# Whole-head values' products of 512 columns, a gate turned by VectorE and probabilities scaled on ScalarE, in the attention stage of a fused diffusion block

## The chip, the cores and the metric

One core of one Trainium2 chip runs the whole block in one launch. The metric is the device time of an execution in microseconds; the kernel before has a median of 1329.95 us over three runs (1327.25 to 1331.77). TensorE multiplies, VectorE and ScalarE work on whole tiles, GpSimd (POOL) and SyncE (SP) issue DMAs, as ScalarE does too.

## The reference, cut to what matters

The input is 512 latent tokens and 256 context tokens, each of 2048 channels. All arithmetic is in float32. The part that the change touches:

```python
q = _rope(_rmsnorm(_heads(p, OFF_Q, N_Q_HEADS), q_norm_g[l]), cos, sin) * q_scale
k = _rope(_rmsnorm(_heads(p, OFF_K, N_KV_HEADS), k_norm_g[l]), cos, sin)
v = _heads(p, OFF_V, N_KV_HEADS)
attn = _attention(q, concatenate([k, kc]), concatenate([v, vc]))   # softmax(q k^T) v, 12 heads, 4 key heads
...
y_a = (attn * jax.nn.silu(z_a)) @ w_pa
y_b = (_fourier_mix(u_b) * jax.nn.silu(z_b)) @ w_pb
return (g_a * y_a + g_b * y_b) @ w_o
```

Ahead of this lies an adaptive normalisation and one input projection of 9216 columns, and behind it a gated residual and a final normalisation. There are 12 query heads of 128 channels, 4 key and value heads, 768 keys. `z_a` is the gate of the attention branch: 12 x 128 channels, one for each of the branch's.

## The kernel before, in words

Float32 precision is kept by splitting each operand into a high and a low part (`split_from`, L162: a copy on ScalarE gives the high part, a subtraction on VectorE the low one) and by three products for each pair (`mm3`, L303). `split_from` is thus one line for many tiles, L163 on ScalarE and L164 on VectorE.

The kernel runs in stages. First come the modulation and the Fourier branch. Then the input projection runs as eight column groups (`KINDS`, L58) by a scheme of seven products of half-size blocks (`Group`, L727). The first three groups each hold queries for four heads (`c` = 0 in `qz_done`, L887) and the gate for the same heads (`c` = 1). The queries are normalised and rotated, turned by VectorE in blocks of 32 x 32 (L872) and written to DRAM (`q_d`). The gate is put through `z * (tanh(z/2) + 1)`, which is twice its SiLU, and written to DRAM by head (`z_d`) with the tokens on the partitions.

The attention stage is a hand-written loop of 48 steps and 3 closing ones (L1220 to L1252). Step `i` works for query tile `t = i % 4` (128 tokens) of head `h = i // 4`:

- `load_head(h + 2)` (L1046) when `t` is 1: the gate by one POOL DMA (L1048), the queries by `load_turned` (L210), which is four SP DMAs whose pieces are 32 floats long (L215). It thereby finishes the transposition that VectorE began within 32 x 32 blocks.
- `scores(i)` (L1147): six products give 128 x 768 scores in PSUM (tag `x`, two buffers of two banks); VectorE takes the row maximum (L1157) and scales it (L1158); ScalarE takes the exponential into a tile `probs` and sums it (L1160).
- `fill(1)`: one unit (three products of 512 columns) of a filler, the Fourier branch's own projection, 64 units in all. A unit is handed out evenly: `want = 3 + 61 * (i + 1) // 48`. Every fourth unit ends with a ScalarE copy out of PSUM (L1134).
- `values` (L1183), in every second step from step 4: 18 products of 256 columns for two query tiles, two steps behind; the same PSUM bank takes two TensorE transposes of the gate (L1191), ScalarE copies those out (L1199) and VectorE multiplies (L1200). Behind the second half of a head the result is split into `S` (L1204), the left operand of the branch's projection.
- `turn(i - 1)` (L1172): six TensorE transposes of the probabilities into PSUM (`tp`, one buffer of two banks), then ScalarE and VectorE split them into `pth` and `ptl`. Two pairs of these buffers exist, each for 256 tokens.
- `divide(i - 1)` (L1164): VectorE takes the reciprocal of the row sum (L1169) and multiplies it into the gate's rows (L1170), not into the probabilities.
- `split_queries(h + 1)` when `t` is 1, and further units of the filler that are owed.

Which instruction stands where on an engine is decided by a scheduler at build time: each engine takes the earliest instruction of the program whose operands and buffers it reckons to be free. The trace shows such shifts: the products of step `i + 2`'s scores stand partly ahead of `turn(i)`. On the chip each engine runs its list in that order. A buffer with one copy makes its next writer wait for its last reader.

After the loop the branch's projection over all heads follows (`products`, L1207), of which six pieces already run in the last steps.

Of the kernel before, what the change touches and what calls it, by code (L numbers as in the profile page):

```python
# [10 lines left out]
F32 = mybir.dt.float32  # L11
F32R = mybir.dt.float32r
ACT = mybir.ActivationFunctionType
ALU = mybir.AluOpType
# [4 lines left out]
P = 128  # L19
D = 2048  # L20
T = 512
C = 256
KK = D // P
HD = 128
NH = 12
NKV = 4
GQ = NH // NKV
NKEY = T + C
KT = NKEY // P
# [29 lines left out]
NQZ, KV = 3, 5  # L59
# [48 lines left out]
def block_kernel(ctx, tc, xT, ctx_rows, ctx_toks, x, c_row, w_ss, w_gate, vecs, qkg, rope, dft_c, dft_s,  # L108
                 w_start, w_g, w_pab, w_o, final_g, out):
    nc = tc.nc  # L110
# [15 lines left out]
    dsc = ctx.enter_context(tc.tile_pool(name="dsc", bufs=1, space=DRAM))  # L126
# [2 lines left out]
    cf_d = dsc.tile([4, P, 7, 2, P], F32, name="cf_d")  # L129
    v_d = dsc.tile([NKV, P, KT, HD], F32, name="v_d")  # L130
    q_d = dsc.tile([NQZ, 4, P, 4 * P], F32, name="q_d")
    z_d = dsc.tile([NH, P, 4, HD], F32, name="z_d")
    b_d = dsc.tile([2, P, 2, T], F32, name="b_d")
    g_d = dsc.tile([2, 2, 4, P, 1024], F32, name="g_d")
    pss, ps = region("ps", None, space=PSUM)
# [3 lines left out]
    def uid(s):  # L139
        cnt[0] += 1  # L140
        return f"{s}{cnt[0]}"
# [20 lines left out]
    def split_from(src, hi, lo):  # L162
        nc.scalar.activation(hi, src, ACT.Copy)  # L163
        return nc.vector.tensor_tensor(lo, src, hi.bitcast(F32), op=ALU.subtract)  # L164
# [45 lines left out]
    def load_turned(dst, src, g):  # L210

        for c in range(4):
            n = P * g + 32 * c
            blocks = src[:, :, n : n + 32].rearrange("t (a i) j -> i (t a) j", a=4)
            nc.sync.dma_start(dst[32 * c : 32 * c + 32].rearrange("i (u j) -> i u j", j=32), blocks)  # L215
# [74 lines left out]
    def slot_tile(p, shape, dt):  # L290
        return p[0].tile([P] + list(shape), dt, tag=p[1], bufs=1, name=uid("s"))

    def take(shape, dt=F32, pool=None):
        p = next((p for p in free if p[0] is pool), free[0])
        free.remove(p)
        t = slot_tile(p, shape, dt)
        home[id(t)] = p, t
        return t

    def give(*ts):  # L300
        free.extend(home.pop(id(t))[0] for t in ts)

    def mm3(o, ah, al, bh, bl, start, stop, cont=False):  # L303

        nc.tensor.matmul(o, ah, bh, start=start, stop=False, skip_group_check=cont)  # L305
        nc.tensor.matmul(o, ah, bl, start=False, stop=False, skip_group_check=cont)  # L306
        nc.tensor.matmul(o, al, bh, start=False, stop=stop, skip_group_check=cont)  # L307


    ident = const.tile([P, P], F32, name="ident")  # L310
# [29 lines left out]
    kept = {}  # L340
# [21 lines left out]
    flat = lambda v: v.rearrange("p t c -> p (t c)")  # L362
# [14 lines left out]
    for g in range(LAST + 1):  # L377
        for name in ONE_GROUP:
# [6 lines left out]
            for pc in range(4):  # L385
                p = context_piece(g, name, pc)
# [12 lines left out]
    S = {}  # L399
# [3 lines left out]
    for name in OUT_GROUP:  # L403
        stream_product(name, 8, w_o[1], BY_DVE_OUT)
        if name in DONE:
            half, c = DONE[name]
# [480 lines left out]
    def qz_done(half, c, v, t):  # L887

        if c:
            e = pair("x" if half else "y")  # L890
            nc.scalar.activation(e, v, ACT.Tanh, scale=0.5)
            nc.vector.scalar_tensor_tensor(v, e, 1.0, v, op0=ALU.add, op1=ALU.mult)
            r = v.rearrange("p t (h d) -> p t h d", h=4)
            for b in range(2):
                nc.scalar.dma_start(z_d[4 * group.g : 4 * group.g + 4, :, 2 * half + b, :].rearrange("h p d -> p h d"), r[:, b])
        else:
            to = q_d[group.g]
            rotated(half, v, lambda: pair("y"), qss[group.g][:, 8 * half : 8 * half + 8], False,
                    lambda t, r: nc.scalar.dma_start(to[t].rearrange("p (h d) -> p h d", h=4), r))
# [14 lines left out]
    class Context:  # L914
# [43 lines left out]
        def values(self, b, v):  # L958
            nc.scalar.dma_start(by_group(v_d[:, :, 4 + b, :]), v.rearrange("p (g d) -> p g d", g=4))
# [84 lines left out]
    qz, qs, kv = {}, {}, {}  # L1044

    def load_head(h):  # L1046
        qz[h] = take((2, T))
        nc.gpsimd.dma_start(qz[h][:, 1, :], flat(z_d[h]))  # L1048
        load_turned(qz[h][:, 0, :], q_d[h // 4], h % 4)

    def get_keys(g):
        keys = get(("K", g))
        kv[g] = tuple(w[:, 0, :] for w in keys) + get(("V", g))
# [6 lines left out]
    for g, kind in enumerate(KINDS):  # L1060
# [8 lines left out]
        group = Group(g, forms, new_ev, {"qz": qz_done, "kv": kv_done, "gate": gate_done}[kind], {"a": "x", "b": "y", "c": "x"})  # L1069
# [36 lines left out]
    ats_, atp = region("atp", "right", reuse_waits="tile")  # L1106
# [5 lines left out]
    ybs, S = {}, {}  # L1112
# [31 lines left out]
    probs, pts, branch = {}, {}, {}  # L1144
    NSTEP = 4 * NH

    def scores(i):  # L1147
        h, t = divmod(i, 4)
        kh, kl = kv[h // GQ][:2]
        s = slice(t * P, (t + 1) * P)  # L1150
        qh, ql = qs[h][:, 0, s], qs[h][:, 1, s]
        sc = flat(pair("x"))
        for a, b in ((0, 512), (512, 768)):
            mm3(sc[:, a:b], qh, ql, kh[:, a:b], kl[:, a:b], True, True)
        mx = stats[:, 4 * (i % 4) : 4 * (i % 4) + 4]
        r = qss[h // 4][:, 4 * t + h % 4 : 4 * t + h % 4 + 1]
        nc.vector.tensor_reduce(mx[:, 0:1], sc[:, :NKEY], axis=AX.X, op=ALU.max, negate=True)  # L1157
        nc.vector.tensor_tensor(mx[:, 0:1], mx[:, 0:1], r, op=ALU.mult)  # L1158
        probs[i] = take((NKEY,))
        nc.scalar.activation(probs[i], sc[:, :NKEY], ACT.Exp, bias=mx[:, 0:1], scale=r, accum_out=mx[:, 1:2])  # L1160
        if t == 3:
            give(qs.pop(h))

    def divide(i):  # L1164

        h, t = divmod(i, 4)
        z = qz[h][:, 1, t * P : t * P + P]
        r = stats[:, 4 * (i % 4) + 2 : 4 * (i % 4) + 3]
        nc.vector.reciprocal(r, stats[:, 4 * (i % 4) + 1 : 4 * (i % 4) + 2])  # L1169
        nc.vector.tensor_scalar(z, z, r, None, op0=ALU.mult)  # L1170

    def turn(i):  # L1172
        p = probs.pop(i)
        tp = flat(psp.tile([P, 2, 512], F32, tag=f"y{turned_y}", bufs=1, name=uid("tp")))
        for k in range(KT):
            nc.tensor.transpose(tp[:, k * P : (k + 1) * P], p[:, k * P : (k + 1) * P], ident)
        if i % 2 == 0:
            pts[i // 2] = [atp.tile([P, KT, 256], F32R, tag=n, bufs=2, name=uid(n)) for n in ("pth", "ptl")]
        c = slice((i % 2) * P, (i % 2) * P + P)
        split_from(tp[:, :NKEY].rearrange("p (k q) -> p k q", k=KT), *(w[:, :, c] for w in pts[i // 2]))  # L1180
        give(p)

    def values(half):  # L1183
        h, second = divmod(half, 2)
        vh, vl = kv[h // GQ][2:]
        pth, ptl = pts.pop(half)
        av = b1()
        for k in range(KT):
            mm3(av[:, :256], vh[:, k, :], vl[:, k, :], pth[:, k, :], ptl[:, k, :], k == 0, k == KT - 1)
        for t in range(2):  # L1190
            nc.tensor.transpose(av[:, 256 + t * P : 256 + (t + 1) * P], qz[h][:, 1, (2 * second + t) * P : (2 * second + t + 1) * P], ident)  # L1191
        if second:
            give(qz.pop(h))
            if h % GQ == GQ - 1:
                give(*kept.pop(h // GQ))
        else:
            branch[h] = take((2, T))
        at, zt = (branch[h][:, i, 256 * second : 256 * second + 256] for i in range(2))
        nc.scalar.copy(zt, av[:, 256:])  # L1199
        nc.vector.scalar_tensor_tensor(at, av[:, :256], 0.5, zt, op0=ALU.mult, op1=ALU.mult)  # L1200
        if second:
            if h % 2 == 0:
                S[h // 2] = [take((2, T), F32R) for _ in range(2)]
            split_from(branch[h][:, 0, :], *(w[:, h % 2, :] for w in S[h // 2]))  # L1204
            give(branch.pop(h))

    def products(j, accs):  # L1207

# [7 lines left out]
                        pc == 0 and k == 0, pc == BRANCH_A[-1] and k == 1)  # L1216
                yield pc, t

    filled = 0
    for i in range(NSTEP + 3):  # L1220
        h, t = divmod(i, 4)
        if i < NSTEP:
            if t == 1 and h + 2 < NH:
                load_head(h + 2)
            if i == 24:
                load_row(0)
            elif i == 28:
                silu_of_row(0)
            if i % 12 == 10 and i // 12 + 1 < NKV:
                get_keys(i // 12 + 1)  # L1230
            scores(i)
        want = min(3 + 61 * (i + 1) // NSTEP, 64)
        if want > filled:
            fill(1)
            filled += 1
        if i % 2 == 0 and i >= 4:
            values((i - 4) // 2)
        if 1 <= i <= NSTEP:
            turn(i - 1)
            divide(i - 1)  # L1240
        if t == 1 and h + 1 < NH:
            split_queries(h + 1)
        if want > filled:
            fill(want - filled)
            filled = want
        if i == NSTEP - 1:
            fill(1)
            first_sums = [pair("x") for _ in range(2)]
            first = products(CHUNKS[0], first_sums)
        if NSTEP > i - 2 >= NSTEP - 3:  # L1250
            next(first)
            next(first)  # L1252
# [353 lines left out]
```

## Time and profile before

| | |
|---|---|
| median of three runs | 1329.95 us |
| profiled execution | 1326.24 us, its span 1324.5 us |
| granted TensorE clock | 0.997 |
| TensorE busy | 1291.6 us, 98% |
| VectorE busy | 983.3 us, 74% |
| ScalarE busy | 657.0 us, 50% |
| attention stage | 828 to 1027 us |

A row of the groups names line, engine, operation, output and inputs by their names in the program, shapes, count, then the busy time in us, the mean of one in ns, and the engine's idle time before them with what ended it. A row of the timeline starts with the start and the length in us, then engine, line, operation and count; a bracket gives the idle time ahead of it. Matmuls are pipelined, so the length of one (0.28 us for 256 columns) is more than the distance to the next one's start. `SPq` and `POOLq` are the queues that issue DMAs. `y<-pth,s` are the values' products, `y<-whi,s` the filler's, `x<-s,s` the scores'. A row of the windows gives the busy time of each engine in a stretch, its count of instructions in brackets, then clock, DMA share and GB/s.

### The profile page before, as it was taken

How to read it: one execution, taken by the hardware profiler on the slowest of the kernel's cores; microseconds unless marked ns; L12 is line 12 of the kernel's file. 1: busy time of each engine (PE TensorE's matmuls, PEld its weight loads, DVE VectorE, ACT ScalarE, POOL GpSimd, SP SyncE). 2: the span in 40 equal slices, each digit the busy share in tenths (PEclk: the TensorE clock that was granted, in tenths of full speed). 3: DMA queues.
4: the chain of work that ended last, by engine and by line, in shares of the span. 5: the costliest groups of instructions: out<-in, count | busy, mean ns of one | idle time of the engine just before them, and what ended most of it. 6: DMA issues, size and time to landing. Idle time of an engine off the chain costs nothing. (4 is left out here: it accounts for less than half of the span.)

```text
span 1324.5 us, 17511 instructions
## 1 busy us (share of the span) xinstructions
PE 1291.6 (98%) x6522; PEld 1053.6 (80%) x6522; DVE 983.3 (74%) x1341; ACT 657.0 (50%) x1018; POOL 136.4 (10%) x186
## 2 busy tenths in 40 slices
PE   7999999999999999999999999999999999999995
PEld 3566888888888887888888888888888888878884
DVE  4655889878777875748487667778776889687677
ACT  5322655555555553544354545767665133364534
POOL 1110011110201111011021010000000100110210
PEclk9999999999999999999999999999999999999999
DMA  9996677887898987977659798432113988778973
GB/s 382 404 383 250 222 194 204 217 231 214 198 306 214 280 275 199 306 180 171 203 153 329 226 220 211 100 90 80 33 49 128 350 346 301 185 155 252 225 204 127
DMA packets 125718, 291.28 MB, mean 220 GB/s; under 512 B 46784, under 2 KB 60608, under 8 KB 121280
## 3 DMA queue, kind: packets, MB, share of 16 engines
q1 hardware_dynamic: 88912, 176.10, 39.7%
q0 software_dynamic: 21168, 91.24, 28.6%
q10 hardware_dynamic: 15552, 22.81, 4.9%
q8 instruction: 51, 0.84, 0.3%
q14 instruction: 35, 0.29, 0.1%
HBM read 263.37 MB, written 26.75 MB: 219 GB/s over the span
## 5 line engine op out<-in xcount | busy, mean ns | idle before, releaser
L163 ACT ACTIVATE whi<-wr 128x1024 fp32r<-128x1024 f32 (+1 forms) x129 | 135.1, 1052 | 180.2 <-PE y L307 77.3
L306 PE MATMUL x<-wlo,s 128*128 128x512 f32 x548 | 214.4, 391 | 4.0 <-DVE wlo L164 4.0
L305 PE MATMUL y<-whi,s 128*128 128x512 f32 x544 | 214.3, 394 | 1.8 <-ACT s L774 1.1
L305 PE MATMUL x<-whi,s 128*128 128x512 f32 x548 | 214.6, 392 | 0.2 <-ACT s L771 0.2
L307 PE MATMUL x<-whi,s 128*128 128x512 f32 x548 | 214.0, 391 | 0.0
L306 PE MATMUL y<-wlo,s 128*128 128x512 f32 x544 | 212.3, 390 | 1.3 <-DVE wlo L164 1.3
L307 PE MATMUL y<-whi,s 128*128 128x512 f32 x544 | 212.3, 390 | 0.0
L164 DVE TENSOR_TENSOR wlo<-wr,whi 128x1024 fp32r<-128x1024 f32 (+1 forms) x129 | 155.6, 1212 | 63.4 <-ACT whi L163 63.0
L163 ACT ACTIVATE whi<-R 128x1024 fp32r<-128x1024 f32 x115 | 121.2, 1059 | 129.5 <-PE x L307 58.5
L164 DVE TENSOR_TENSOR wlo<-R,whi 128x1024 fp32r<-128x1024 f32 x115 | 140.0, 1221 | 48.7 <-ACT whi L163 48.5
L306 PEld LDWEIGHTS x<-wlo,s 128*128 128x128 f32 x548 | 103.2, 188 | 26.3 <-DVE wlo L164 5.1
L305 PEld LDWEIGHTS y<-whi,s 128*128 128x128 f32 x544 | 102.2, 188 | 24.4 <-DVE s L1200 2.8
L305 PEld LDWEIGHTS x<-whi,s 128*128 128x128 f32 x548 | 103.3, 189 | 22.1 <-ACT s L771 0.5
L307 PEld LDWEIGHTS x<-whi,s 128*128 128x128 f32 x548 | 103.2, 188 | 21.5
L307 PEld LDWEIGHTS y<-whi,s 128*128 128x128 f32 x544 | 102.1, 188 | 21.6
L306 PEld LDWEIGHTS y<-wlo,s 128*128 128x128 f32 x544 | 102.2, 188 | 20.5 <-DVE wlo L164 1.7
L306 PE MATMUL x<-s,s 128*128 128x512 f32 (+1 forms) x284 | 106.7, 376 | 0.0
L307 PE MATMUL x<-s,s 128*128 128x512 f32 (+1 forms) x284 | 105.9, 373 | 0.0
L305 PE MATMUL x<-s,s 128*128 128x512 f32 (+1 forms) x274 | 104.0, 379 | 0.9 <-ACT s L1160 0.9
L261 POOL DMA_DIRECT2D R<-in_w_g x64 | 55.4, 865 | 435.0 <-DVE wlo L164 319.2
L163 ACT ACTIVATE s<-wr 128x512 fp32r<-128x512 f32 (+2 forms) x98 | 64.3, 679 | 52.7 <-PE y L306 14.0
L164 DVE TENSOR_TENSOR s<-wr,s 128x512 fp32r<-128x512 f32 (+2 forms) x98 | 71.2, 752 | 20.9 <-ACT s L163 19.9
(274 smaller groups left out, 2246.0 us busy)
## 6 DMA issues: line engine op xcount, KB each, us to landing
wr<-in_w_g SPq DMA_DIRECT2D x128, 512.0 KB, 4.7
R<-in_w_g POOLq DMA_DIRECT2D x64, 512.0 KB, 7.0
wa<-in_w_ss POOLq DMA_DIRECT2D x28, 1024.0 KB, 9.1
R<-in_w_g SPq DMA_DIRECT2D x32, 512.0 KB, 5.1
wr<-in_w_pab SPq DMA_DIRECT2D x32, 512.0 KB, 5.0
wr<-in_w_gate SPq DMA_DIRECT2D x32, 512.0 KB, 5.4
wr<-in_w_o SPq DMA_DIRECT2D x24, 512.0 KB, 5.4
R<-in_w_o POOLq DMA_DIRECT2D x24, 512.0 KB, 7.4
```

The costliest lines, as they stand in the source:

```text
L163: nc.scalar.activation(hi, src, ACT.Copy)
L164: return nc.vector.tensor_tensor(lo, src, hi.bitcast(F32), op=ALU.subtract)
L261: nc.gpsimd.dma_start(chain[e.pc], e.nxt, accum_op=ALU.add)
L305: nc.tensor.matmul(o, ah, bh, start=start, stop=False, skip_group_check=cont)
L306: nc.tensor.matmul(o, ah, bl, start=False, stop=False, skip_group_check=cont)
L307: nc.tensor.matmul(o, al, bh, start=False, stop=stop, skip_group_check=cont)
```

## The change

The gate now leaves the projection stage already turned in blocks of 32 x 32 by VectorE (into the tile `v`, from PSUM), is stored in the same layout as the queries and loaded by `load_turned`, that is by four SP DMAs of short pieces in place of one POOL DMA of 2 KB rows. TensorE's transposes of the gate and ScalarE's copies of them are gone.

`divide` is called at the end of `scores` and multiplies the reciprocal of the row sum into the probabilities, 128 x 768, on ScalarE; before, VectorE multiplied it into the gate, 128 x 128.

`values` runs once a head, in every fourth step from step 5, with 18 products of 512 columns. `pth` and `ptl` are one pair of buffers for 512 tokens in place of two pairs for 256: the same space. One VectorE multiplication takes a whole head's result.

The filler's units are weighted: a step with values counts 2, the others 3.

```diff
-    z_d = dsc.tile([NH, P, 4, HD], F32, name="z_d")
+    z_d = dsc.tile([NQZ, 4, P, 4 * P], F32, name="z_d")
...
             nc.scalar.activation(e, v, ACT.Tanh, scale=0.5)
-            nc.vector.scalar_tensor_tensor(v, e, 1.0, v, op0=ALU.add, op1=ALU.mult)
-            r = v.rearrange("p t (h d) -> p t h d", h=4)
+            nc.vector.scalar_tensor_tensor(e, e, 1.0, v, op0=ALU.add, op1=ALU.mult)
+            nc.vector.transpose(flat(v), flat(e))
             for b in range(2):
-                nc.scalar.dma_start(z_d[4 * group.g : 4 * group.g + 4, :, 2 * half + b, :].rearrange("h p d -> p h d"), r[:, b])
+                nc.scalar.dma_start(z_d[group.g, 2 * half + b], v[:, b])
...
     def load_head(h):
         qz[h] = take((2, T))
-        nc.gpsimd.dma_start(qz[h][:, 1, :], flat(z_d[h]))
         load_turned(qz[h][:, 0, :], q_d[h // 4], h % 4)
+        load_turned(qz[h][:, 1, :], z_d[h // 4], h % 4)
...
         nc.scalar.activation(probs[i], sc[:, :NKEY], ACT.Exp, bias=mx[:, 0:1], scale=r, accum_out=mx[:, 1:2])
+        divide(i)
...
     def divide(i):
 
-        h, t = divmod(i, 4)
-        z = qz[h][:, 1, t * P : t * P + P]
         r = stats[:, 4 * (i % 4) + 2 : 4 * (i % 4) + 3]
         nc.vector.reciprocal(r, stats[:, 4 * (i % 4) + 1 : 4 * (i % 4) + 2])
-        nc.vector.tensor_scalar(z, z, r, None, op0=ALU.mult)
+        nc.scalar.mul(probs[i], probs[i], r)
...
-        if i % 2 == 0:
-            pts[i // 2] = [atp.tile([P, KT, 256], F32R, tag=n, bufs=2, name=uid(n)) for n in ("pth", "ptl")]
-        c = slice((i % 2) * P, (i % 2) * P + P)
-        split_from(tp[:, :NKEY].rearrange("p (k q) -> p k q", k=KT), *(w[:, :, c] for w in pts[i // 2]))
+        h, t = divmod(i, 4)
+        if t == 0:
+            pts[h] = [atp.tile([P, KT, T], F32R, tag=n, bufs=1, name=uid(n)) for n in ("pth", "ptl")]
+        c = slice(t * P, t * P + P)
+        split_from(tp[:, :NKEY].rearrange("p (k q) -> p k q", k=KT), *(w[:, :, c] for w in pts[h]))
         give(p)
 
-    def values(half):
-        h, second = divmod(half, 2)
+    def values(h):
         vh, vl = kv[h // GQ][2:]
-        pth, ptl = pts.pop(half)
+        pth, ptl = pts.pop(h)
         av = b1()
         for k in range(KT):
-            mm3(av[:, :256], vh[:, k, :], vl[:, k, :], pth[:, k, :], ptl[:, k, :], k == 0, k == KT - 1)
-        for t in range(2):
-            nc.tensor.transpose(av[:, 256 + t * P : 256 + (t + 1) * P], qz[h][:, 1, (2 * second + t) * P : (2 * second + t + 1) * P], ident)
...
+            mm3(av, vh[:, k, :], vl[:, k, :], pth[:, k, :], ptl[:, k, :], k == 0, k == KT - 1)
+        at = take((T,))
+        nc.vector.scalar_tensor_tensor(at, av, 0.5, qz[h][:, 1, :], op0=ALU.mult, op1=ALU.mult)
...
-    filled = 0
+    filled, weigh = 0, [2 if i > 4 and i % 4 == 1 else 3 for i in range(NSTEP)]
...
-        want = min(3 + 61 * (i + 1) // NSTEP, 64)
+        want = 3 + 61 * sum(weigh[: i + 1]) // sum(weigh)
...
-        if i % 2 == 0 and i >= 4:
-            values((i - 4) // 2)
+        if i % 4 == 1 and i > 4:
+            values(i // 4 - 1)
         if 1 <= i <= NSTEP:
             turn(i - 1)
-            divide(i - 1)
```

More of the change, by code (lines that the diff above doesn't have):

```diff
@@ L1176, in turn @@
             nc.tensor.transpose(tp[:, k * P : (k + 1) * P], p[:, k * P : (k + 1) * P], ident)
-        if i % 2 == 0:
-            pts[i // 2] = [atp.tile([P, KT, 256], F32R, tag=n, bufs=2, name=uid(n)) for n in ("pth", "ptl")]
-        c = slice((i % 2) * P, (i % 2) * P + P)
-        split_from(tp[:, :NKEY].rearrange("p (k q) -> p k q", k=KT), *(w[:, :, c] for w in pts[i // 2]))
+        h, t = divmod(i, 4)
[3 more added lines that the diff above has]
+        split_from(tp[:, :NKEY].rearrange("p (k q) -> p k q", k=KT), *(w[:, :, c] for w in pts[h]))
         give(p)
-    def values(half):
-        h, second = divmod(half, 2)
+    def values(h):
         vh, vl = kv[h // GQ][2:]
-        pth, ptl = pts.pop(half)
+        pth, ptl = pts.pop(h)
         av = b1()
         for k in range(KT):
-            mm3(av[:, :256], vh[:, k, :], vl[:, k, :], pth[:, k, :], ptl[:, k, :], k == 0, k == KT - 1)
-        for t in range(2):
[L1191 to L1205, printed above, removed]
+            mm3(av, vh[:, k, :], vl[:, k, :], pth[:, k, :], ptl[:, k, :], k == 0, k == KT - 1)
+        at = take((T,))
+        nc.vector.scalar_tensor_tensor(at, av, 0.5, qz[h][:, 1, :], op0=ALU.mult, op1=ALU.mult)
+        give(qz.pop(h))
+        if h % GQ == GQ - 1:
+            give(*kept.pop(h // GQ))
+        if h % 2 == 0:
+            S[h // 2] = [take((2, T), F32R) for _ in range(2)]
+        split_from(at, *(w[:, h % 2, :] for w in S[h // 2]))
+        give(at)
     def products(j, accs):
```

## The prediction

> **What bounds the kernel now.** I read the page's busy shares first, then the busy time of each engine over the attention stage (828 to 1027 us, from the first score products to the last values' products).
>
> ```profile
> span 1324.5 us, 17511 instructions
> PE 1291.6 (98%) x6522; PEld 1053.6 (80%) x6522; DVE 983.3 (74%) x1341; ACT 657.0 (50%) x1018; POOL 136.4 (10%) x186
> ```
>
> ```profile
> 828.00:1027.00 199.00, 195.91 (x1283) 171.36 (x1282) 148.65 (x301) 129.97 (x222) 7.04 (x14) 1.00 0.30 80
> ```
>
> TensorE is occupied in 195.91 of these 199 us (columns: PE, PEld, DVE, ACT, POOL, clock, DMA share, GB/s). It sets the pace: 3.1 us of the stage are idle, and VectorE (148.65) and ScalarE (129.97) have room on average. The profiled execution took 1326.24 us, 1.74 around its span, and lies 3.7 below the median of the three runs, 1329.95. I work out a difference on the profile and put it on the median.
>
> The groups of the stage, shapes kept apart (busy us, mean ns of one | idle before):
>
> ```profile
> L1160 ACT ACTIVATE s<-x,gain,small 128x768 f32<-128x768 f32 x48 | 47.6, 992 | 19.9 <-DVE gain L1158 17.2 <-DVE s L1170 1.5 <-DVE gain L1169 1.2
> L164 DVE TENSOR_TENSOR ptl<-tp,pth 128x768 fp32r<-128x768 f32 x48 | 45.9, 955 | 15.2 <-ACT pth L163 14.9
> L305 PE MATMUL y<-pth,s 128*128 128x256 f32 x144 | 40.8, 283 | 0.0
> L163 ACT ACTIVATE pth<-tp 128x768 fp32r<-128x768 f32 x48 | 38.9, 811 | 23.9 <-PE tp L1176 23.7
> L305 PE MATMUL x<-s,s 128*128 128x512 f32 x47 | 20.7, 440 | 0.9 <-ACT s L1160 0.9
> L1170 DVE TENSOR_SCALAR s<-s,gain 128x128 f32<-128x128 f32 x48 | 13.7, 286 | 1.0
> L1200 DVE SCALAR_TENSOR_TENSOR s<-y,s 128x256 f32<-128x256 f32 x24 | 10.1, 422 | 8.3 <-ACT s L1199 8.3
> L1191 PE MATMUL y<-ident,s 128*128 128x128 f32 x48 | 9.1, 271 | 0.0
> L1199 ACT COPY s<-y 128x256 f32<-128x256 f32 x24 | 8.9, 370 | 14.7 <-PE y L1191 14.7
> L163 ACT ACTIVATE s<-wr 128x768 fp32r<-128x768 f32 x4 | 3.4, 844 | 0.8 <-PE x L307 0.5 <-DVE s L164 0.3
> ```
>
> The durations of products overlap (283 ns for 256 columns, 440 for 512), so their cost is the distance of starts. From the timeline, one half head's 18 values' products with the two transposes of the gate, and score products of both widths:
>
> ```profile
> 926.38 0.28 PE L305 MATMUL y<-pth,s 128*128 128x256 f32 x1
> ...
> 928.52 0.38 PE L1191 MATMUL y<-ident,s 128*128 128x128 f32 x2
> ...
> 928.74 0.82 PE L1176 MATMUL tp<-ident,s 128*128 128x128 f32 x6
> ...
> 929.63 0.39 PE L306 MATMUL x<-s,s 128*128 128x512 f32 x1
> ...
> 929.86 0.40 PE L307 MATMUL x<-s,s 128*128 128x512 f32 x1
> ...
> 930.09 0.28 PE L305 MATMUL x<-s,s 128*128 128x256 f32 x1
> ```
>
> 18 products of 256 columns from 926.38 to 928.52: 119 ns each. 512 columns: 929.63 to 929.86 to 930.09, 230 ns each. The two gate transposes hold TensorE from 928.52 to 928.74, 0.22 us.
>
> **1. What TensorE saves.** Values' products: 24 x 18 x 0.119 = 51.4 us now; 12 x 18 x 0.231 = 49.9 after. Twice the columns take nearly twice the time, so this is worth 1.5 us (0.9 to 2, by 2 to 7 ns of spread in the starts). Gate transposes: 24 x 0.22 = 5.3 us, at most the 9.1 us of their group's busy time. Together 6 to 11 us, about 7 if nothing new makes TensorE wait.
>
> A rule here says more. The Trainium skill, "TensorE: Matmul & The Clock Gate", section "Back-to-back issue gap", gives sustained spacings of about 81 ns for 128 columns and 131 for 512; a straight line between gives an estimate of 98 for 256, so 42.3 us would fall to 28.3, a gain of 14. This trace's 119 and 230 disagree, and I go by them.
>
> **2. What ScalarE and VectorE get.** Leaving ScalarE: 24 copies, 8.9 us. Coming: 48 scalings of 128x768. No row shows one with a per-partition factor; the plain 768 copy takes 844 ns, the exponential with two per-partition operands 992. I take 0.92, between them: 44 us (40.5 to 47.6). ScalarE goes from 130 to 165 of 199 us. VectorE loses 13.7 us of gate divisions and trades 24 x 0.422 for 12 of twice the width, at most twice as long: 149 to about 135. A scaling now stands between exponential and transposes, with the reciprocal and hand-overs some 1.3 us. Queued behind it on ScalarE are the next split of turned probabilities (pth), the filler's copies and the weight splits. The section "Rules for kernel authors" of "ScalarE: Activation LUTs" in the Trainium skill says to put multiplications on VectorE, not ScalarE; that is the direction in which this term is dangerous.
>
> **3. The new chain.** Now each half head has its own pair of pth/ptl buffers, two pairs deep, so values' products run while later steps are being split. After, there is one pair of whole-head size. A head's first split waits until all 18 products of the head before have read the pair, and those 18 wait for that head's last split. The turned tile tp is single already: transposes, pth on ScalarE, ptl on VectorE, then the next transposes. So for each head there is a serial chain: 18 products, then four times (transposes, pth, ptl). One clean round, from the timeline:
>
> ```profile
> 841.50 0.99 ACT L1160 ACTIVATE s<-x,gain,small 128x768 f32<-128x768 f32 x1 [0.70 <-DVE gain L1158]
> ...
> 843.00 0.82 PE L1176 MATMUL tp<-ident,s 128*128 128x128 f32 x6
> ...
> 843.86 0.81 ACT L163 ACTIVATE pth<-tp 128x768 fp32r<-128x768 f32 x1 [0.28 <-PE tp L1176]
> ...
> 844.70 0.96 DVE L164 TENSOR_TENSOR ptl<-tp,pth 128x768 fp32r<-128x768 f32 x1 [0.67 <-ACT pth L163]
> ...
> 845.72 0.88 PE L1176 MATMUL tp<-ident,s 128*128 128x128 f32 x6
> ...
> 1003.01 0.60 PE L1176 MATMUL tp<-ident,s 128*128 128x128 f32 x4
> ```
>
> A round is 845.72 - 843.00 = 2.72 us when nobody is late. 843.00 is the start of turn 3, 845.72 of turn 4 and 1003.01 of turn 44, so a head takes (1003.01 - 845.72) / 10 = 15.73 us now. After, the chain needs 18 x 0.231 + 4 x 2.72 = 15.04 us at least: only 0.69 under what a head takes now, all TensorE's saving. Each 0.17 us that a round is longer uses it up. The scaling itself needn't lengthen a round: turn 4's exponential ended at 842.49, 3.2 us ahead of its transposes, and 1.3 fits; ScalarE being occupied when pth is due does.
>
> How late is it today? The first and the last of 48 turns, and a bad one:
>
> ```profile
> 831.16 0.76 PE L1176 MATMUL tp<-ident,s 128*128 128x128 f32 x5 [0.50 <-ACT s L1160]
> ...
> 832.46 0.27 PE L1176 MATMUL tp<-ident,s 128*128 128x128 f32 x1
> ...
> 832.93 0.80 ACT L163 ACTIVATE pth<-tp 128x768 fp32r<-128x768 f32 x1
> ...
> 833.76 0.96 DVE L164 TENSOR_TENSOR ptl<-tp,pth 128x768 fp32r<-128x768 f32 x1 [0.22 <-ACT pth L163]
> ```
>
> ```profile
> 1016.51 0.82 PE L1176 MATMUL tp<-ident,s 128*128 128x128 f32 x6
> ...
> 1017.37 0.81 ACT L163 ACTIVATE pth<-tp 128x768 fp32r<-128x768 f32 x1 [0.28 <-PE tp L1176]
> ...
> 1018.21 0.96 DVE L164 TENSOR_TENSOR ptl<-tp,pth 128x768 fp32r<-128x768 f32 x1 [0.67 <-ACT pth L163]
> ```
>
> ```profile
> 912.75 0.82 PE L1176 MATMUL tp<-ident,s 128*128 128x128 f32 x6
> ...
> 914.77 0.80 ACT L163 ACTIVATE pth<-tp 128x768 fp32r<-128x768 f32 x1
> ```
>
> From the end of the transposes to pth: 0.20 us in the first, 0.04 in the last, 1.20 in the bad one, 0.197 on average over the 48. From the end of pth to ptl: 0.03 in the first and the last, 0.185 on average. A clean round holds 0.04 and 0.03 of these, so the average round has 0.31 extra. Today that mostly costs nothing, since TensorE has other work; on the new chain it counts. Scaling the first with ScalarE's other work (130 - 39 = 91 us now, 165 - 39 = 126 after) gives 0.27, the second with VectorE's (103 to 88) gives 0.16: 0.36 extra. A head then takes 4.16 + 4 x 3.08 = 16.48 us, 0.75 more than now. Over the 11 distances from the first to the last head's products that is +8.3 us; the twelfth head keeps TensorE's saving of 0.6. **Sum: +8 us.** With no extra it is 11 x (15.04 - 15.73) - 0.6 = -8, which is the gain of part 1 again; with twice the extra +24.
>
> **4. The rest, at nothing.** The gate's six VectorE transposes lie in the projection stage:
>
> ```profile
> L872 DVE STREAM_TRANSPOSE qr<-y x7: 1236/1243/1250, 217.5 to 692.7; 128x1024 f32<-128x1024 f32 x7
> ```
>
> ```profile
> 220.00:410.00 190.00, 189.97 (x838) 157.00 (x837) 155.53 (x180) 103.40 (x191) 26.41 (x27) 1.00 0.81 231
> ```
>
> 6 x 1.24 = 7.5 us, in 34 us of VectorE's idle time beside a TensorE that never waits there, its weights split ahead. If that cover failed, up to 7.5. The gate's loads move from POOL to SP, four small ones for one: 48 more at 0.49 us, 23 us of SP spread over the stage, and 2048 more small packets a head where the DMA share is 0.30. The first two heads' are the tight ones (SP's group, then the timeline):
>
> ```profile
> L215 SPq DMA_DIRECT2D s<-q_d x48: 302/486/1650, 768.3 to 963.7; - x48
> ```
>
> ```profile
> 772.72 6.33 SPq L215 DMA_DIRECT2D s<-q_d  x7
> 785.62 0.35 SPq L202 DMA_DIRECT2D wr<-in_w_g  x1
> ```
>
> Eight more at 0.9 us fill the 6.6 us that SP stands idle behind them and delay the next weight load by about 1 us; it was waiting for VectorE anyway. The gate is wanted only at a head's values. Nothing to +2.
>
> **The rivals.** *Faster: the rounds stay clean.* The four rounds repeat alike, VectorE is lighter, and 4.2 us of values' products per head let ScalarE run exponentials and scalings ahead. If the extra stays under 0.08 us a round, TensorE remains the bound: -7 us, 1323. Against it: the 0.31 of today, with ScalarE less loaded. *No change:* 0.08 to 0.26 extra, the saving is eaten and no more: 1326 to 1334. *ScalarE becomes the bound:* between two heads' values it would have four splits, three or four exponentials and scalings and a head's weight splits and copies in 11 us; the extra goes to 0.7 or more, 1350 and above. *A fixed price per product:* if the durations in the groups were the price, 432 x 0.283 would become 216 x 0.391 at best, -38 us, about 1290; the distances of starts exclude it almost wholly. The TensorE page's spacings quoted in part 1 would give, with the transposes, -20 us. *The change doesn't do what it says* has no room: the products of 512 columns exist in the trace, as do the loads by blocks.
>
> **How the numbers follow.** Forecast (extra above 0.26 us a round): 0.47, of which 0.10 is ScalarE as the bound; no change 0.23; faster 0.30, of which 0.02 the fixed price. The predicted time is 1329.95 + 8 = 1338. The forecast's own range is 1334 to 1350. The whole range reaches down to the clean rounds, 1322, and up to 1350; some 0.17 lie outside. 0.3%, about 4 us, is what a measurement can tell from no change.
>
> **What would show it.** Right: values' products of 512 columns at 230 ns from start to start; ScalarE near 165 us in the stage; TensorE waiting at its transposes or at the values for ptl, 10 us or more; from one head's values to the next over 16 us. Wrong: the distance from head to head at 15.1 to 15.3 with TensorE's idle time unchanged (the rounds stay clean); products of 512 columns at much under 230 ns; waits of TensorE in the projection stage, which would put the loss on the gate's transposes or on SP.

## The result, and the profile after

The changed kernel takes 1351.49 us (median of four runs, 1346.25 to 1353.26) against 1328.6 for the kernel before on the same chip. The ratio is 1.016, 95% interval 1.0137 to 1.0183: 21 us slower by the ratio, 18 to 24 (the two medians lie 22.9 apart). The forecast was slower by 8, with a range that ended at 1350. The profiled execution took 1346.25 us, 20.0 more than the one before, and 5.2 less than its kernel's median.

From the page, the span and the busy shares; then the windows view of the attention stage, which now runs from 832 to 1044 us:

```profile
span 1344.5 us, 16952 instructions
PE 1293.7 (96%) x6258; PEld 1040.6 (77%) x6258; DVE 976.7 (73%) x1287; ACT 689.2 (51%) x1042; POOL 129.4 (10%) x174
```

```profile
832.00:1044.00 212.00, 193.97 (x1000) 154.41 (x999) 136.53 (x241) 161.45 (x246) 0.55 (x1) 0.99 0.31 75
```

TensorE is busy for 194 of 212 us: 18 us of the stage are idle where 3.1 were before. No engine is full: VectorE 137, ScalarE 161. From the start of the first row maximum to the start of the last values' product the stage takes 212.4 us (831.73 to 1044.17) against 197.6 (827.03 to 1024.67), so 14.8 of the profile's 20 us arise there.

The groups that changed (busy us, mean ns | idle before):

```profile
L1169 ACT ACTIVATE s<-s,gain 128x768 f32<-128x768 f32 x48 | 44.9, 935 | 7.6 <-DVE gain L1168 7.5
L305 PE MATMUL y<-pth,s 128*128 128x512 f32 x72 | 29.2, 406 | 2.4 <-ACT pth L163 2.4
L305 PE MATMUL x<-s,s 128*128 128x512 f32 x47 | 21.3, 453 | 11.7 <-ACT s L1160 11.6
L1190 DVE SCALAR_TENSOR_TENSOR s<-y,s 128x512 f32<-128x512 f32 x11 | 7.6, 692 | 18.2 <-PE y L307 18.1
```

A scaling takes 935 ns on ScalarE (0.92 was forecast). VectorE stands idle 18.1 us ahead of the values' multiplication, waiting for products: averaged over ten heads, it is busy in 1.25 of the 4.2 us of a block of products, and ScalarE in 2.8. TensorE's longest wait is at the scores' first product, for an exponential to free a score buffer. The waits view of the stage:

```profile
PE x L305 <- ACT s L1160: 11.6, 13, 2.6
PE y L305 <- ACT pth L163: 2.4, 3, 1.2
```

One head of the timeline around its values (columns: start, length, engine, line, tiles, what it waited for):

```profile
1004.92 0.85 PE L1175 MATMUL tp<-ident,s 128*128 128x128 f32 x6 [0.28 <-DVE gain L1158]
...
1005.87 0.80 ACT L163 ACTIVATE pth<-tp 128x768 fp32r<-128x768 f32 x1
...
1006.70 0.96 DVE L164 TENSOR_TENSOR ptl<-tp,pth 128x768 fp32r<-128x768 f32 x1 [0.54 <-ACT pth L163]
...
1006.93 0.39 PE L305 MATMUL y<-pth,s 128*128 128x512 f32 x1
...
1007.71 0.50 PE L306 MATMUL y<-ptl,s 128*128 128x512 f32 x1 [0.16 <-DVE ptl L164]
...
1011.56 0.39 PE L307 MATMUL y<-pth,s 128*128 128x512 f32 x1
1011.79 0.60 PE L1175 MATMUL tp<-ident,s 128*128 128x128 f32 x4
```

This is the chain link by link: the head's last transposes, pth, ptl, the products as soon as ptl is there (the first needs only pth and slips in early), and the next head's first transposes right behind the last product (in eight of the ten heads from turn 4 to 44; in the other two they stand some 4 us earlier). From 1007.71 to 1011.56 lie 16 distances of starts, 17 products, 0.24 us each.

Turn 4 and turn 44, ten heads apart, from the timeline:

```profile
853.94 0.49 PE L1175 MATMUL tp<-ident,s 128*128 128x128 f32 x3
...
1027.90 0.49 PE L1175 MATMUL tp<-ident,s 128*128 128x128 f32 x3
```

(1027.90 - 853.94) / 10 = 17.40 us a head, against 15.73 before and 16.48 forecast. This head distance is the measure used below.

### The profile page after: what moved, and what is told of

Its sections match the earlier page's. It is cut to its first block, busy times and chain, and to the rows that moved or that the text cites. A ratio compares the mean times of both kernels' runs of the same rounds, so it can differ in the third digit from the quotient of the medians.

```text
span 1344.5 us, 16952 instructions
## 1 busy us (share of the span) xinstructions
PE 1293.7 (96%) x6258; PEld 1040.6 (77%) x6258; DVE 976.7 (73%) x1287; ACT 689.2 (51%) x1042; POOL 129.4 (10%) x174
## 5 line engine op out<-in xcount | busy, mean ns | idle before, releaser
L306 PE MATMUL y<-wlo,s 128*128 128x512 f32 x544 | 212.4, 390 | 0.0
L164 DVE TENSOR_TENSOR wlo<-wr,whi 128x1024 fp32r<-128x1024 f32 (+1 forms) x129 | 155.4, 1211 | 59.8 <-ACT whi L163 59.5
L164 DVE TENSOR_TENSOR wlo<-R,whi 128x1024 fp32r<-128x1024 f32 x115 | 139.8, 1219 | 51.7 <-ACT whi L163 51.7
L164 DVE TENSOR_TENSOR s<-wr,s 128x512 fp32r<-128x512 f32 (+2 forms) x98 | 71.0, 750 | 18.9 <-ACT s L163 18.8
```

## The experiments

Theory A: the one whole-head pair of pth and ptl makes a serial chain of products and four rounds, and that chain sets the distance from head to head. Theory B: ScalarE's 48 scalings are the cause whatever the buffers. Two pairs for whole heads, which need twice the space, were not tried. The first four runs tell them apart. "Before" is the kernel before on the same chip.

**Half heads again.** The changed kernel with the values of the kernel before; the gate by VectorE and the scaling on ScalarE stay. Three things go back together: the two pairs of buffers, the products of 256 columns and the even handing-out of the filler. The run with one pair, below, takes the first of them alone.

```diff
-            pts[h] = [atp.tile([P, KT, T], F32R, tag=n, bufs=1, ...
+            pts[i // 2] = [atp.tile([P, KT, 256], F32R, tag=n, bufs=2, ...
...
-        if i % 4 == 1 and i > 4:
-            values(i // 4 - 1)
+        if i % 2 == 0 and i >= 4:
+            values((i - 4) // 2)
```

> The changed kernel with its values' products put back to half heads of 256 columns, two pairs of pth/ptl and the even filler; the gate turned by VectorE and the scaling on ScalarE stay. Theory A (the serial chain through the one whole-head pair sets the distance from head to head): the chain is gone, a head takes 15.7 us or less, 1323 to 1333 us. Theory B (ScalarE's 48 scalings are the cause): nothing much returns, 1342 to 1352.

1330.96 us, ratio 0.9999 (0.9986 to 1.0012). The loss is gone with the scaling still in place. The head distance, and the stage's windows row, in which ScalarE is as busy as in the changed kernel (161):

```profile
852.60 0.49 PE L1175 MATMUL tp<-ident,s 128*128 128x128 f32 x3
...
1007.72 0.52 PE L1175 MATMUL tp<-ident,s 128*128 128x128 f32 x3
```

```profile
833.00:1030.00 197.00, 190.36 (x1231) 167.18 (x1231) 138.19 (x255) 160.94 (x246) 1.08 (x2) 1.00 0.35 84
```

15.51 us a head.

**No scaling.** The changed kernel without line 1169; the reciprocals stay and nothing is divided by the row sum.

```diff
-        nc.scalar.mul(probs[i], probs[i], r)
```

> The changed kernel with the scaling of the probabilities left out (it leaves out the division by the row sum; the reciprocals stay). Theory A: the chain stays, only its rounds are less late: 16.5 to 17 us a head, 1338 to 1347 us. Theory B: all of the loss returns, 1320 to 1330.

1339.16 us, ratio 1.0057 (1.0037 to 1.0077). The chain alone, net of what TensorE saves, costs 8 us (5 to 10); the scaling on the chain costs the other 13 to 14.

```profile
853.38 0.49 PE L1174 MATMUL tp<-ident,s 128*128 128x128 f32 x3
...
1015.97 0.49 PE L1174 MATMUL tp<-ident,s 128*128 128x128 f32 x3
```

16.26 us a head: +0.53 over before, and the scaling adds 1.14.

**One pair in the kernel before.**

```diff
-            pts[i // 2] = [atp.tile([P, KT, 256], F32R, tag=n, bufs=2, name=uid(n)) for n in ("pth", "ptl")]
+            pts[i // 2] = [atp.tile([P, KT, 256], F32R, tag=n, bufs=1, name=uid(n)) for n in ("pth", "ptl")]
```

> The kernel before with one pair of half-head pth/ptl buffers in place of two, nothing else. Theory A: the same kind of chain without any scaling: per head 2 x 2.36 (18 products and the gate's transposes) + 4 x 3.03 = 16.8 us against 15.73, so +12 us, 1336 to 1346. Theory B: no change beyond 4 us.

1345.98 us, ratio 1.011 (1.0087 to 1.0132). No scaling, no other change, and two thirds of the loss. Here the wait stands in the open, since the transposes come ahead of the products:

```profile
1010.39 0.82 PE L1176 MATMUL tp<-ident,s 128*128 128x128 f32 x6
...
1011.74 0.28 PE L305 MATMUL y<-pth,s 128*128 128x256 f32 x1
...
1013.76 0.28 PE L307 MATMUL y<-pth,s 128*128 128x256 f32 x1
...
1014.14 0.81 ACT L163 ACTIVATE pth<-tp 128x768 fp32r<-128x768 f32 x1 [1.89 <-PE y L307]
```

The transposes are done at 1011.21, pth starts at 1014.14, 0.1 us after the last product ended. In the bracket is what it waited for. Its heads:

```profile
857.59 0.49 PE L1176 MATMUL tp<-ident,s 128*128 128x128 f32 x3
...
1026.68 0.49 PE L1176 MATMUL tp<-ident,s 128*128 128x128 f32 x3
```

16.91 us a head, where the chain gave 16.8. That these two agree so well is partly luck: the transposes of every second turn are done before the products end and aren't on the chain, and from the end of the last ptl to the second product 1.4 us pass on average (ten heads, two halves each), in which TensorE mostly works through other products and transposes that stand ahead in its list; neither was in the expectation.

**The scaling alone in the kernel before.**

```diff
-        nc.vector.tensor_scalar(z, z, r, None, op0=ALU.mult)
+        nc.scalar.mul(probs[i], probs[i], r)
```

(with `divide` called from `scores`)

> The kernel before with the division moved from the gate on VectorE to the probabilities on ScalarE, nothing else. Theory A: two pairs leave TensorE other work, so within 5 us of the kernel before, 1325 to 1335. Theory B: +15 us or more, 1343 and above.

1329.66 us, ratio 0.9991 (0.9977 to 1.0005). With two pairs, 48 scalings on ScalarE cost nothing. Theory B has fallen; the scaling costs on the chain only. The next question was what of it costs there: that ScalarE is occupied (A1), or that the scaling stands between exponential and transposes (A2).

**The load without the place.** The scalings write to a tile nobody reads; nothing is divided.

```diff
-        nc.scalar.mul(probs[i], probs[i], r)
+        nc.scalar.mul(idle[0], probs[i], r)
```

> The changed kernel in which ScalarE's 48 scalings write to a tile that nobody reads (so the probabilities aren't divided): ScalarE's load stays, the step between exponential and transposes is gone. Theory A1 (on the chain ScalarE's occupation costs: it is in a scaling when a split or an exponential is due): 1347 to 1354 us, as the changed kernel. Theory A2 (the scaling's place between exponential and transposes costs): 1336 to 1343, as without a scaling.

1348.91 us, ratio 1.0142 (1.0119 to 1.0165). A scaling takes as long as before (936 ns in the middle). Its heads:

```profile
852.96 0.49 PE L1176 MATMUL tp<-ident,s 128*128 128x128 f32 x3
...
1027.89 0.49 PE L1176 MATMUL tp<-ident,s 128*128 128x128 f32 x3
```

17.49 us a head, no less than the changed kernel's 17.40. So it is the occupancy: A1 holds.

**The scaling on VectorE, whole heads.**

```diff
-        nc.scalar.mul(probs[i], probs[i], r)
+        nc.vector.tensor_scalar(probs[i], probs[i], r, None, op0=ALU.mult)
```

> The changed kernel with the scaling of the probabilities on VectorE, whole-head pair kept. Theory A1: ScalarE is as free as without a scaling, VectorE has some 25 to 45 us more: 1339 to 1347 us, between the kernel without scaling and the changed one. Theory A2: the step is still between exponential and transposes, 1345 to 1352.

1343.69 us, ratio 1.0101 (1.0081 to 1.012); 16.33 us a head ((1022.05 - 858.76) / 10). A scaling takes 617 ns there. The chain stays and ScalarE's share of the loss is gone from the heads. It isn't gone from the total as clearly: the kernel without scaling has nearly the same heads (16.26) and a ratio of 1.0057. In this profile the stage takes 204.8 us, 7.1 more than before, and begins 9.2 us later, at 836.2; where the other 6 us or so of its time come from stays open.

**Half heads with the scaling on VectorE,** the version that these runs point to: the edits of the first and the last together.

> Half heads with two pairs as in the first run, the gate turned by VectorE, and the scaling on VectorE. If ScalarE's load ate the saving of the gate's transposes (5 us of TensorE) in the first run, some of it comes back: 1324 to 1331 us against 1331. If VectorE is then the one that is late: 1331 to 1338.

1328.9 us, ratio 0.9996 (0.998 to 1.0011). In its profile a head takes 15.32 us ((1003.93 - 850.70) / 10) and the stage 193.6, 4.0 less than before, but the total isn't told apart from the kernel before. No version here beats it.

**Half heads with the scaling on GpSimd.**

> The same with the scaling on GpSimd, which is nearly idle in the stage. If one scaling takes under 2 us there, it is hidden: 1324 to 1331 us. If it takes 3 us or more, or slows VectorE's own work, the transposes wait for it: 1340 and above.

1345.15 us, ratio 1.0112 (1.0094 to 1.013). From the views of the groups by line and of the waits:

```profile
L1169 POOL TENSOR_SCALAR s<-s,gain x48: 2196/2206/2711, 837.8 to 1033.5; 128x768 f32<-128x768 f32 x48
```

```profile
PE tp L1175 <- POOL s L1169: 13.5, 16, 1.4
```

One scaling takes 2.2 us there, between the two cases of the expectation (under 2, or 3 and more), and TensorE waits for it at the transposes, 13.5 us in all. VectorE's own work isn't slowed: its subtraction (L164) takes 953 ns, the same as with the scaling on ScalarE. So here the place between exponential and transposes does cost: 2.2 us are too long, 0.94 are not.

**The two halves of the gate's move, added to the kernel before.** First its six VectorE transposes in the projection stage, their result not used:

```diff
             nc.vector.scalar_tensor_tensor(v, e, 1.0, v, op0=ALU.add, op1=ALU.mult)
+            nc.vector.transpose(flat(e), flat(v))
```

> The kernel before with the gate's six VectorE transposes added in the projection stage, their result not used (the gate goes on as before). If VectorE's idle time there hides them, as the prediction had it: within 3 us of the kernel before. If the projection pays for them: up to +7.5 us.

1331.14 us, ratio 1.0019 (1.0004 to 1.0033): 0.5 to 4.4 us. In the window from 220 to 410 us VectorE is busy 162.95 us instead of 155.53 and TensorE 189.98 of 190, so no wait of TensorE in the profile shows where they are paid. Then the SP loads:

```diff
+        load_turned(qz[h][:, 0, :], q_d[h // 4], h % 4)
+        load_turned(qz[h][:, 1, :], q_d[h // 4], h % 4)
         nc.gpsimd.dma_start(qz[h][:, 1, :], flat(z_d[h]))
-        load_turned(qz[h][:, 0, :], q_d[h // 4], h % 4)
```

> The kernel before with four more SP loads of short pieces for each head (they are overwritten by the gate's own load): the SP and DMA load of the new way to fetch the gate, on top of the old one. If they are hidden: within 3 us of the kernel before. If the weights behind them on SP come late: TensorE waits between 770 and 1020 us and the time is 5 us or more longer.

1330.78 us, ratio 1.0007 (0.9991 to 1.0024): no cost to be seen, at most 3 us.

**The changed kernel again.**

> The changed kernel a second time. Its profiled execution was 5 us under its median; if the stage's length varies with the share of the clock that is granted, this profile shows a stage over 212 us with more windows at half clock; if not, the stage is again 212 to 213 us and the spread lies ahead of it.

1352.03 us, ratio 1.0173 (1.0151 to 1.0195). The stage took 214.6 us this time, and a head 17.57 us ((1032.20 - 856.48) / 10). Two windows of its stage (the column before the last two is the granted clock):

```profile
885.00:898.00 13.00, 10.55 (x46) 8.55 (x47) 7.50 (x13) 9.01 (x14) 0.00 (x0) 0.87 0.12 19
940.00:953.00 13.00, 10.84 (x48) 8.50 (x48) 8.06 (x13) 8.38 (x14) 0.00 (x0) 0.87 0.18 29
```

0.13 x 13 = 1.7 us of clock lost in each, that is 3.4 us at half speed. The first profile has one such stretch in the stage, the kernel before none. One stretch more, 1.7 us, is what ten heads took longer here (17.57 against 17.40).

## Why the prediction was right or wrong

**The mechanism was right.** The forecast's case was the serial chain, and the runs show it: one pair in the kernel before, with nothing else changed, brings 16.91 us a head against 15.73 and two thirds of the loss; in the changed kernel two pairs (with the narrower products) take the loss away. Parts 1 and 2 held too. A values' product of 512 columns takes 0.23 to 0.24 us, so the wide products gain next to nothing. The 14 us that the prediction worked out from "Back-to-back issue gap" of "TensorE: Matmul & The Clock Gate" in the Trainium skill didn't appear. A scaling takes 0.935 us (0.92), and ScalarE's stage 161 us (165). The advice of "ScalarE: Activation LUTs", section "Rules for kernel authors", in the Trainium skill to multiply on VectorE and not on ScalarE holds here on the chain (16.33 us a head against 17.40) and makes no difference that the time shows off it (half heads: 0.9999 with the scaling on ScalarE, 0.9996 on VectorE).

**The size failed at one step**, in part 3: "Scaling the first with ScalarE's other work ... gives 0.27, the second with VectorE's ... gives 0.16: 0.36 extra. A head then takes 4.16 + 4 x 3.08 = 16.48". 17.40 were measured. The mis-sized term is the extra of a round: 0.59 us ((17.40 - 4.16) / 4 - 2.72) in place of 0.36. Averaged over 40 turns of the changed kernel, pth is 0.28 us late (0.27 forecast), ptl 0.24 (0.16), and from the end of ptl to the next transposes inside a head 0.22 us pass (0.06). This last wait was given no extra at all, without a reason; it makes up 0.49 of the 0.92 us a head that were missing, and ptl 0.31.

The agreement at pth is luck, and so is part of another one: without the scaling the same sum gives 16.28 us a head, and 16.26 were measured. The kernel without scaling shows what lies behind it. There pth, behind the first turn of a head, is only 0.08 us late, less than the 0.20 that were carried over from the kernel before, and the wait ahead of the transposes is 0.20, almost as long as with the scaling. One error made up for the other. The third wait thus belongs to the chain: TensorE is mostly still in a product of the scores or the filler that stands ahead of the transposes in its list.

The scaling was given 4 x 0.05 = 0.2 us a head and takes 1.14. Of this 0.84 lie at pth (0.36 us late in place of 0.08, in the three turns of a head that follow its first) and 0.41 at ptl; the third wait grew by 0.08, and the products begin 0.28 sooner behind the last ptl. Up to 0.17 of the 1.14 can be the clock: ten heads of the changed kernel hold one stretch at half speed, which those of the kernel without scaling don't. The lateness at pth grew more than fourfold, and not with ScalarE's other work (126 us in the stage against 91), because it comes in few turns: eight of the 40, in which pth stands behind a scaling in ScalarE's list (twice with a split of weights in between), hold 8.4 of the 11.1 us. One of them:

```profile
862.95 0.85 PE L1175 MATMUL tp<-ident,s 128*128 128x128 f32 x6
...
863.50 1.05 ACT L163 ACTIVATE whi<-wr 128x1024 fp32r<-128x1024 f32 x1
...
864.45 0.93 ACT L1169 ACTIVATE s<-s,gain 128x768 f32<-128x768 f32 x1
...
865.28 0.80 ACT L163 ACTIVATE pth<-tp 128x768 fp32r<-128x768 f32 x1
```

The transposes end at 863.80, and pth starts 1.48 us later. Over the stage, ten head distances bring 16.7 us, and its two ends give 1.9 back.

**What was expected as a sign** came so in part. TensorE waits 18 us in the stage, as said, but mostly at the scores and not at the transposes or the values. ScalarE as the bound, the rival of 1350 and more, had the time and half of the picture: ScalarE's lateness costs the larger part of the loss, but ScalarE isn't the bound. Averaged over ten heads it is busy in 10.3 of the 13.0 us between two blocks of products, and the extra is 0.59 us a round where the rival said 0.7 or more.

**Part 4.** The SP loads show no cost (0.9991 to 1.0024). The VectorE transposes, put at nothing, or at up to 7.5 us if their cover failed, cost 0.5 to 4.4. The gate's transposes that TensorE is spared, 5 us in part 1, brought little: in the runs on half heads the head distance fell from 15.61 with the scaling alone ((1010.57 - 854.43) / 10) to 15.51 with the gate moved as well. Only with the scaling on VectorE is the stage 4.0 us shorter than before.

**What the profiles don't settle.** Of the 20 us between the two first profiles 4.7 lie ahead of the stage. Nothing shows that these are an effect of the change: most of them lie between 440 and 560 us, where the kernel with the scaling alone, its gate as before, waits as long as the changed one (changed kernel first; 5.2 and 6.1 of 120 us idle, the profile before 2.9) and the granted clock is 0.97 in both (0.99 before). In the four profiles whose gate is as before, the stage begins anywhere from 827.0 to 837.0 us:

```profile
440.00:560.00 120.00, 114.79 (x495) 94.46 (x494) 85.77 (x129) 57.89 (x81) 7.59 (x9) 0.97 0.89 275
```

```profile
440.00:560.00 120.00, 113.91 (x491) 93.73 (x490) 84.74 (x129) 57.72 (x81) 8.40 (x10) 0.97 0.87 267
```

The times differ by 21 us by the ratio, the stages by 14.8 and, in the second profile, 16.9; the gate's transposes on VectorE account for some 2 more. About 2 to 4 us stay unplaced.

## What to carry to other kernels

Before making a buffer larger by taking away its second copy, write down the chain it closes (who must have read it before it is written, who must have written it before it is read) and compare its length with what a turn of the loop takes now: here 15.04 us against 15.73 left 0.17 us a round, and the waits already in the trace used it up. Add the waits link by link, from a trace in which the chain is closed if there is one: an average scaled by an engine's load missed that few turns hold most of the lateness. The same 0.94 us of ScalarE's work a step was free with two copies (0.9991) and cost 13 to 14 us with one. Cost wider products by the distances of their starts, not by their durations.

## What the runs showed of the hardware

- The same 128x768 multiplication by one factor per partition takes 617 ns on VectorE, 935 on ScalarE and 2206 (median) on GpSimd.
- A long idle time of TensorE can cost twice: in the changed kernel's stage the granted clock fell to half for 3.4 us once or twice in an execution, 1.7 us of clock each time, which no profile of the kernel before shows in this stage. In the first profile the stretch begins at 917.4 us, with this product behind 1.90 us of idle time:

```profile
917.16 0.58 PE L305 MATMUL x<-s,s 128*128 128x512 f32 x1 [1.90 <-ACT s L1160]
```

"TensorE: Matmul & The Clock Gate", section "Part 1: The HAM clock gate", of the Trainium skill gives the half clock as the state after at least one idle window of about 3.4 us. The length of the stretches agrees with that window; the condition doesn't, since TensorE was idle for only 1.90 us ahead of this one. Not every such time is followed by a stretch: two others in the same stage, of 2.65 and 2.16 us, are not. The stage with the scaling on GpSimd, idle for 18.8 us in pieces of at most 1.42, has none.
